# A 4-byte write per partition put between two large loads on the SyncE queue of an RMSNorm kernel

## The chip, the cores and the metric

One core of one Trainium2 chip. The metric is device time in microseconds (us) of one execution, median of the runs. A kernel's profile is one execution; its "span" is counted from the first to the last instruction and is about 1.9 us shorter than the time. All profiles told of here are of the undisturbed ("fast") state, with a granted TensorE clock of 1.0.

Engines: ACT is ScalarE, DVE is VectorE, PE is TensorE, SP is SyncE, POOL is GpSimd. An "SPq" line is the sequencer of SyncE, which issues the DMAs of this kernel. The DMA work itself is done by 16 DMA engines.

Three words are used throughout. A "piece" is one contiguous run of elements in a DMA; the profile counts one packet for each. The "ring" of a DMA engine is the list of packets that it works through. A DMA has "landed" when the trace shows the semaphore event of its completion.

## The reference

```python
x: (16, 1024, 512) float32, gamma: (512,) float32
rms = sqrt(mean(x ** 2, axis=-1, keepdims=True) + 1e-5)
out = x / rms * gamma
```

33.55 MB come in and 33.55 MB go out. The 16384 rows are cut into 4 tiles; in a tile each of the 128 partitions holds 32 whole rows (64 KB, contiguous in memory).

## The kernel before

Three slots of 64 KB per partition; tiles 0, 1, 2 have a slot each and tile 3 uses slot 0 again after tile 0 is stored. All large DMAs are on the SyncE queue.

```python
    def load(t, slot, r0, r1):
        nc.sync.dma_start(out=slots[slot][:, r0:r1], in_=xv[t][:, r0:r1])
    def store(t, slot, r0, r1):
        nc.sync.dma_start(out=ov[t][:, r0:r1], in_=slots[slot][:, r0:r1])

    load(0, 0, 0, 16)
    load(0, 0, 16, 32)
    load(1, 1, 0, 32)
    load(2, 2, 0, 32)
    # ... (gamma broadcast over the partitions, eps) cut
    # compute(slot, r0, r1), per 8 rows: ACT squares (and sums half of the groups itself,
    # the other half through PSUM and a DVE reduce, L74), ACT sqrt, DVE reciprocal,
    # then 8 DVE scalar_tensor_tensor (L88), one per row: slot = slot * rstd * gamma. Cut.
    compute(0, 0, 32)
    store(0, 0, 0, 32)
    compute(1, 0, 16)
    store(1, 1, 0, 16)
    load(3, 0, 0, 16)
    load(3, 0, 16, 32)
    compute(1, 16, 32)
    store(1, 1, 16, 32)
    compute(2, 0, 32)
    store(2, 2, 0, 32)
    compute(0, 0, 16)
    store(3, 0, 0, 16)
    compute(0, 16, 32)
    store(3, 0, 16, 32)
```

## Time and profile before

| | before |
|---|---|
| time, median (lowest to highest) of the first three runs | 162.51 us (162.43 to 162.78) |
| span of the profile | 160.6 us |
| DVE busy, ACT busy | 123.4 us (77%), 79.9 us (50%) |
| share of the 16 DMA engines' span used by the SyncE queue | 97.9% |

From the page of the kernel before: the count of DMA packets, the queues (packets, MB, share of 16 engines), and the chain of work that ended last, as shares of the span.

```profile
span 160.6 us, 402 instructions
PE 2.0 (1%) x2; PEld 0.5 (0%) x2; DVE 123.4 (77%) x163; ACT 79.9 (50%) x162; POOL 0.2 (0%) x4
...
DMA packets 1732, 67.13 MB, mean 418 GB/s; under 512 B 193, under 2 KB 193, under 8 KB 194
## 3 DMA queue, kind: packets, MB, share of 16 engines
q1 hardware_dynamic: 1728, 67.11, 97.9%
...
DVE 71%; ACT 12%; DMA 8%; issue 1%; DVEq 0%
```

The chain says DVE and the queue table says DMA. Both are nearly full, which is why neither may be read alone. The next view is the timeline of SyncE's issues before (start, us from the first to the end of the last of a merged group, engine and line, what, how many).

```profile
0.73 1.95 SPq L42 DMA_DIRECT2D slot<-in_x_dram  x4
50.09 23.33 SPq L45 DMA_DIRECT2D out_dram<-slot  x2
82.24 0.84 SPq L42 DMA_DIRECT2D slot<-in_x_dram  x2
88.31 59.93 SPq L45 DMA_DIRECT2D out_dram<-slot  x4
```

All four loads are queued by 2.7 us, store(0) follows at 50.1 us, and the last store is issued at about 147.9 us (88.31 + 59.93, less its own 0.34). The landing times in the trace's semaphore events show one unbroken stream: 12.80 and 22.48 us for the halves of load(0), 41.84 for load(1), 62.83 for load(2), 82.17 for store(0), and so on to 149.89 and 159.55 for the last two stores. Store(0) was issued at 50.1 us and found the engines busy with load(2) until 62 us.

The last view is of ACT between 22 and 60 us before: only the instructions ahead of which ACT stood idle; in brackets, for how long, and what ended it.

```profile
39.26 0.30 ACT L85 ACTIVATE rms<-ss,eps_t 128x8 f32<-128x8 f32 x1 [5.76 <-DVE ss L74]
41.86 0.63 ACT L79 ACTIVATE sq_scratch<-slot 128x512 f32<-128x512 f32 x1 [2.30 <-DMA slot<-in_x_dram]
52.30 1.88 ACT L73 ACTIVATE sq<-slot 128x2048 f32<-128x2048 f32 x1 [4.88 <-DVE ss L74]
```

ACT waits for load(1) at 41.86 us. Afterwards it waits another 4.88 us for DVE. So load(1) could come up to about 4.9 us later and only shorten that second wait. This is the slack of load(1).

### The profile page before, as it was taken

How to read it: one execution, taken by the hardware profiler on the slowest of the kernel's cores; microseconds unless marked ns; L12 is line 12 of the kernel's file. 1: busy time of each engine (PE TensorE's matmuls, PEld its weight loads, DVE VectorE, ACT ScalarE, POOL GpSimd, SP SyncE). 2: the span in 40 equal slices, each digit the busy share in tenths (PEclk: the TensorE clock that was granted, in tenths of full speed). 3: DMA queues.
4: the chain of work that ended last, by engine and by line, in shares of the span. 5: the costliest groups of instructions: out<-in, count | busy, mean ns of one | idle time of the engine just before them, and what ended most of it. 6: DMA issues, size and time to landing. Idle time of an engine off the chain costs nothing.

```text
span 160.6 us, 402 instructions
## 1 busy us (share of the span) xinstructions
PE 2.0 (1%) x2; PEld 0.5 (0%) x2; DVE 123.4 (77%) x163; ACT 79.9 (50%) x162; POOL 0.2 (0%) x4
## 2 busy tenths in 40 slices
PE   4000000000000000000000000000000000000000
PEld 1000000000000000000000000000000000000000
DVE  0101909999999509999999999998999999998000
ACT  3008999930580999995099314003998960000000
POOL 0000000000000000000000000000000000000000
DMA  7999999969969997997999999999997997999993
GB/s 262 392 408 498 400 408 506 522 261 522 522 263 522 506 278 345 441 522 310 473 392 416 465 416 416 473 416 408 457 547 310 506 490 310 416 465 408 433 457 155
DMA packets 1732, 67.13 MB, mean 418 GB/s; under 512 B 193, under 2 KB 193, under 8 KB 194
## 3 DMA queue, kind: packets, MB, share of 16 engines
q1 hardware_dynamic: 1728, 67.11, 97.9%
q14 instruction: 2, 0.02, 0.0%
q10 hardware_dynamic: 2, 0.00, 0.0%
HBM read 33.56 MB, written 33.55 MB: 418 GB/s over the span
## 4 chain that ended last, share of the span: by engine, by line
DVE 71%; ACT 12%; DMA 8%; issue 1%; DVEq 0%
DVE slot L88 52%; DVE ss L74 18%; DMA slot<-in_x_dram 8%; ACT sq_scratch L79 6%; ACT sq L73 4%; DVE rstd L86 1%; ACT L85 1%; ACT rms L85 1%; DVEq L136 0%
## 5 line engine op out<-in xcount | busy, mean ns | idle before, releaser
L88 DVE SCALAR_TENSOR_TENSOR slot<-slot,rstd,gamma_b 128x512 f32<-128x512 f32 x128 | 85.7, 746 | 0.1
L79 ACT ACTIVATE sq_scratch<-slot 128x512 f32<-128x512 f32 x64 | 40.0, 625 | 13.9 <-DMA slot<-in_x_dram 12.6
L74 DVE TENSOR_REDUCE ss<-sq 128x4 f32<-128x2048 f32 x16 | 36.1, 2276 | 10.5 <-ACT sq L73 10.4
L73 ACT ACTIVATE sq<-slot 128x2048 f32<-128x2048 f32 x16 | 29.8, 1860 | 4.9 <-DVE ss L74 4.9
L85 ACT ACTIVATE rms<-ss,eps_t 128x8 f32<-128x8 f32 x16 | 4.4, 297 | 37.4 <-DVE ss L74 37.2
L79 ACT ACTIVATION_READ_ACCUMULATOR sq_scratch<-slot 128x1 f32 x64 | 11.9, 187 | 0.0
L86 DVE RECIPROCAL rstd<-rms 128x8 f32<-128x8 f32 x16 | 2.8, 188 | 9.8 <-ACT rms L85 9.8
L59 DVE COPY gamma_b<-sq 128x512 f32<-128x512 f32 x1 | 0.7, 692 | 3.2 <-PE sq L57 3.2
L57 PE MATMUL sq<-gamma_row,ones_col 1*128 1x512 f32 x2 | 2.0, 1122 | 2.2 <-DMA gamma_row<-in_gamma_dram 2.2
L79 ACT ACT_TABLE_LOAD x1 | 1.3, 1283 | 1.3 <-PEq L125 1.3
L85 ACT ACT_TABLE_LOAD x1 | 1.3, 1283 | 0.0
L55 DVE MEMSET ones_col<- 1x128 f32 x1 | 0.2, 165 | 0.8 <-PEq L125 0.8
L57 PEld LDWEIGHTS sq<-gamma_row,ones_col 1*128 1x128 f32 x2 | 0.5, 305 | 2.1 <-issue 2.1
L125 POOL MEMSET const-bfloat16-1.0<- 128x1 bf16 x1 | 0.1, 102 | 0.0
L125 POOL MEMSET const-uint8-127<- 128x1 uint8 x1 | 0.1, 102 | 0.0
L125 POOL MEMSET const-float32-0.0<- 128x1 f32 x1 | 0.1, 99 | 0.2 <-issue 0.2
L125 POOL MEMSET const-float32-1.0<- 128x1 f32 x1 | 0.1, 99 | 0.0
L62 DVE MEMSET eps_t<- 128x1 f32 x1 | 0.1, 59 | 0.0
## 6 DMA issues: line engine op xcount, KB each, us to landing
slot<-in_x_dram SPq DMA_DIRECT2D x4, 4096.0 KB, 19.3
out_dram<-slot SPq DMA_DIRECT2D x4, 4096.0 KB, 18.0
slot<-in_x_dram SPq DMA_DIRECT2D x2, 50.5
out_dram<-slot SPq DMA_DIRECT2D x2, 27.6
gamma_row<-in_gamma_dram ACTq DMA_DIRECT2D x1, 2.0 KB
```

The source lines that it names most:

```text
L55: nc.vector.memset(ones_col, 1.0)
L57: nc.tensor.matmul(gamma_psum[:, 0], ones_col, gamma_row, start=True, stop=True)
L59: nc.vector.tensor_copy(out=gamma_b, in_=gamma_psum[:, 0])
L62: nc.vector.memset(eps_t, eps)
L73: nc.scalar.activation(out=sq, in_=slots[slot][:, g + h : g + h + H, :], func=AF.Square)
L74: nc.vector.tensor_reduce(out=ss[:, h : h + H], in_=sq, axis=mybir.AxisListType.X, op=OP.add)
L79: nc.scalar.activation(out=sq_scratch, in_=slots[slot][:, g + r, :], func=AF.Square, accum_out=ss[:, r : r + 1],)
L85: nc.scalar.activation(out=rms, in_=ss, func=AF.Sqrt, bias=eps_t, scale=1.0 / D)
L86: nc.vector.reciprocal(out=rstd, in_=rms)
L88: nc.vector.scalar_tensor_tensor(out=slots[slot][:, g + r, :], in0=slots[slot][:, g + r, :], scalar=rstd[:, r : r + 1], in1=gamma_b, op0=O ...
L125: nc = _bacc.Bacc("TRN2", target_bir_lowering=False, num_devices=1)
```

## The change

One constant element (0.0) is written to the first element of each partition's first row of `out`, on the SyncE queue, behind the loads of the first tile and ahead of the second's. store(0) overwrites all of it later, so the result is the same. It adds work and removes none; a reason for it could be to touch `out` early.

```diff
     load(0, 0, 0, 16)
     load(0, 0, 16, 32)
+    nc.sync.dma_start(out=ov[0][:128, 0, 0:1], in_=nc.const_aps.tensor(0.0, [128, 1], fp32), allow_slow_non_contiguous=True)
     load(1, 1, 0, 32)
     load(2, 2, 0, 32)
```

The order of the instructions on PE, ACT, DVE and POOL is the same in both kernels. SyncE has one issue more, and the DMA semaphores are shared out one place further.

## The prediction

> **What bounds the kernel now.** Two things nearly tie. The DMA queue table gives the SyncE queue (q1) 97.9% of the 16 engines' span, and the windows table shows 419 to 433 GB/s in nearly every stretch of 5 us. In the DMA packet records each engine runs its packets back to back from about 1.7 us to 158.5-159.2 us of a 160.6 us span (32 KB took 1.213 us, 64 KB 2.418 us, 27.1 GB/s an engine, 434 GB/s for 16; the Trainium skill, "DMA: Bandwidth & Descriptors", "Where 436 GB/s comes from", states 435, and this trace agrees). The landings are one stream: load(0) halves 12.8 and 22.5 us, load(1) 41.8, load(2) 62.8, store(0) 82.2, and so on to 159.6. The second bound is VectorE: the chain of waits is DVE 71% of the span, DVE is busy almost without a pause from 24 to 147.9 us, and the last store is issued at 147.9. The last 12.7 us is that store. When it reached the DMA engines, four of 16 had been idle 0.06 to 0.2 us; the other twelve were still finishing the store before it. So DMA leads by a hair.
>
> **What the change adds.** One DMA of 128 pieces of 4 B, 8 pieces on each engine, queued behind load(0) and ahead of load(1). No instruction of ACT, DVE, PE or POOL moves; on SyncE one issue is added (0.34 to 0.58 us each in the timeline) far ahead of need. Semaphores shift by one: store(0) also waits for the little write, done long before; load(3)'s first half also waits for a semaphore that gamma used, done too. No new late wait. store(0) overwrites the elements, so the result stands.
>
> **Cost.** The trace has no small HBM write. Its 4 B semaphore packets take 9 ns, the 2 KB gamma packet 98 ns. An estimate from these is 8 x (9 to 60) ns = 0.1 to 0.5 us on each ring. The skill (same page, "Specifications") says that below 512 B the DMA does read-modify-write; no run here shows it yet. If each piece waited out a memory round trip it would be several us; I give that little chance.
>
> A possible gain: the last packet of load(2) on every engine took 3.4 to 3.95 us instead of 2.42, just as the first store's packets come up (58-61.5 us), and the later change from load to store (110 us) shows nothing. If that is a cost of the first write to out, the little write meets it at 22 us instead. I expect it to move, not vanish. If it vanished, the last store is still released by DVE at 147.9, so at most about 0.7 us is gained (159.2 down to 158.5).
>
> **On the critical path.** load(1) may come 4.9 us later before it hurts compute (ACT stalls 4.9 us on DVE afterwards, at 52.3 us), load(2) more. But the rings hold a backlog all the way, so ring time added at 22 us arrives one for one at the end: +0.1 to 0.5 us.
>
> **Prediction.** 162.7 us, 80% range 161.7 to 164.0. Faster by over 2%: 0.02; within 2%: 0.91; slower by over 2%: 0.07.
>
> **What would show it.** Little packets at about 22 us, under 0.5 us per engine in sum; load(1) and all later landings up to 140 us shifted by the same 0.1 to 0.5 us; DVE times from 24 to 147.9 us unchanged within 0.1 us; the long packets at 58 us gone and a similar stall at 22 us.
>
> **What would make it wrong.** Small writes served one by one at a memory round trip (stream moves by several us; beyond 4.9 us DVE slips too); the stall at 58 us vanishing for nothing; the small write upsetting the even spread over engines.

## The result

| | before | after |
|---|---|---|
| time, median (lowest to highest) of 4 runs | 162.58 us (162.43 to 162.78) | 162.40 us (162.33 to 162.87) |
| ratio after / before | | 0.9994, 95% interval 0.9972 to 1.0017: same |
| span of the profile | 160.6 us | 160.6 us |

Ratios here and below are the mean time of one kernel's fast runs over that of the other's fast runs of the same rounds, so they are not quite the ratio of the medians quoted. A second job of the changed kernel with more rounds is told under the experiments.

The same lines of the page, after:

```profile
span 160.6 us, 403 instructions
PE 2.0 (1%) x2; PEld 0.5 (0%) x2; DVE 123.4 (77%) x163; ACT 80.0 (50%) x162; POOL 0.2 (0%) x4
...
DMA packets 1876, 67.13 MB, mean 418 GB/s; under 512 B 337, under 2 KB 337, under 8 KB 338
## 3 DMA queue, kind: packets, MB, share of 16 engines
q1 hardware_dynamic: 1872, 67.11, 97.8%
...
DVE 71%; ACT 12%; DMA 7%; issue 1%; DVEq 0%
```

The reader should see 144 more packets, all under 512 B: 128 pieces of 4 B and 16 semaphore writes, that is 8 and 1 on each engine. SyncE's issues and ACT's waits, after:

```profile
0.73 0.86 SPq L42 DMA_DIRECT2D slot<-in_x_dram  x2
1.64 0.42 SPq L49 DMA_DIRECT2D out_dram<-const-float32-0.0  x1
2.11 1.03 SPq L42 DMA_DIRECT2D slot<-in_x_dram  x2
50.08 23.35 SPq L45 DMA_DIRECT2D out_dram<-slot  x2
...
39.25 0.30 ACT L86 ACTIVATE rms<-ss,eps_t 128x8 f32<-128x8 f32 x1 [5.75 <-DVE ss L75]
41.87 0.63 ACT L80 ACTIVATE sq_scratch<-slot 128x512 f32<-128x512 f32 x1 [2.31 <-DMA slot<-in_x_dram]
52.28 1.88 ACT L74 ACTIVATE sq<-slot 128x2048 f32<-128x2048 f32 x1 [4.86 <-DVE ss L75]
```

The extra issue takes 0.42 us of SyncE, 19 us before the DMA engines come to it; nothing waits for it. In the packet records each of the small packets took 9 ns, 0.08 us for the 9 of one engine. The little write landed at 22.66 us, 0.17 us behind the second half of load(0), and load(1) at 41.85 us, against 41.84 before. ACT's wait behind it is 4.86 us instead of 4.88.

One thing in the packet records answers to a claim of the prediction. Packets of 64 KB take 2.418 us each, but before the change the last packet of load(2) on every engine, which starts at about 58 us, took 1.33 us longer on average (0.95 to 1.53 us on single engines), just as store(0) comes up behind it. After the change it is 1.21 us longer, at the same place, and no packet near 22 us is lengthened. The stall was not moved by the little write.

### The profile page after: what moved, and what is told of

Its sections match the earlier page's. It is cut to its first block, busy times and chain, and to the rows that moved or that the text cites. A ratio compares the mean times of both kernels' runs of the same rounds, so it can differ in the third digit from the quotient of the medians.

```text
span 160.6 us, 403 instructions
## 1 busy us (share of the span) xinstructions
PE 2.0 (1%) x2; PEld 0.5 (0%) x2; DVE 123.4 (77%) x163; ACT 80.0 (50%) x162; POOL 0.2 (0%) x4
## 4 chain that ended last, share of the span: by engine, by line
DVE 71%; ACT 12%; DMA 7%; issue 1%; DVEq 0%
DVE slot L89 52%; DVE ss L75 18%; DMA slot<-in_x_dram 7%; ACT sq_scratch L80 6%; ACT sq L74 4%; DVE rstd L87 1%; ACT L86 1%; ACT rms L86 1%; DVEq L137 0%
```

## The experiments

Theory A, after the result: the stream of DMA packets is packed from end to end, and the write costs its ring time of 0.08 us. Rivals: the write is hidden because DMA has slack; or small writes cost much more than 9 ns, and the first few were only hidden. All kernels gave the right result except the last, which is wrong. Each job also ran the kernel before on the same chip; its medians were 162.61 (first job), 162.73 (second) and 162.52 us (third).

### a1_after_again: the changed kernel again

No edit.

> The changed kernel again, in more rounds. Theory A (a backlogged DMA stream; the little write costs its ring time of 9 packets x 9 ns = 0.08 us per engine, as the trace of after shows): 162.5 to 162.7 us, ratio 1.000 to 1.002. Rival B (the little write changes the stream for the better or worse by something that the packets do not show): a ratio off 1 by more than 0.3%. The long last packets of load(2) at 58 us stay.

Measured: 162.47 us (6 runs) against 162.61 us, ratio 0.9992, interval 0.9977 to 1.0006. Load(1) landed at 41.84 us. The long last packets of load(2) were there (1.22 us over). So the write changes nothing down to about 0.2%.

### e5_head: the same write ahead of the first load

```diff
+    nc.sync.dma_start(out=ov[0][:128, 0, 0:1], in_=nc.const_aps.tensor(0.0, [128, 1], fp32), allow_slow_non_contiguous=True)
     load(0, 0, 0, 16)
     load(0, 0, 16, 32)
```

> The same little write of one element per row, ahead of the first load instead of behind it. Theory A: the first load is issued one SyncE issue (0.42 us in the trace of after) later, so both the DMA stream and the chain of ACT and DVE begin 0.4 us later, and the total is 162.9 to 163.1 us; position matters, not the write itself. Rival: the write is free anywhere, 162.5 us.

Measured: 162.86 us, ratio 1.0019 (1.0005 to 1.0033). SyncE's issues in this kernel:

```profile
0.72 0.37 SPq L47 DMA_DIRECT2D out_dram<-const-float32-0.0  x1
1.15 1.92 SPq L42 DMA_DIRECT2D slot<-in_x_dram  x4
50.68 23.33 SPq L45 DMA_DIRECT2D out_dram<-slot  x2
```

The first load is issued at 1.15 instead of 0.73 us, its first half landed at 13.40 instead of 12.80 us, and DVE released store(0) 0.6 us later. The total rose by 0.25 us between the medians, less than the 0.4 us expected, with the sign expected. Of the two places tried, the added issue cost something at the head, where the first load waits behind it, and nothing measurable behind load(0). The first half came 0.60 us later and the issue accounts for 0.42 us of that; the rest is not explained.

### e1_dose32 and e2_dose128: more pieces in the same place

```diff
+    nc.sync.dma_start(out=ov[0][:128, 0, 0:64:2], in_=nc.const_aps.tensor(0.0, [128, 32], fp32), allow_slow_non_contiguous=True)
```

(and `0:256:2` with `[128, 128]` in e2). Every second element is written, so each is a piece of 4 B: 256 and 1024 pieces on each engine.

> 32 elements per row in place of one: 256 pieces of 4 B on each engine. Theory A (ring time, 9 ns apiece, backlog until the end): 256 x 9 ns = 2.3 us of packets on each engine at 22 us; load(1) lands at 44.1 instead of 41.85 us; DVE times unchanged (slack of 4.9 us); everything in the stream up to the last store 2.2 us later; total 162.5 + 2.2 = 164.7 us. Rival C (DVE alone bounds the kernel, DMA has slack): stays at 162.5 us. Rival D (small writes beyond a few are served at a memory round trip, the first 8 were only hidden): much more than 2.3 us, over 10 us.

> 128 elements per row: 1024 pieces of 4 B on each engine. Theory A: 1024 x 9 ns = 9.2 us; load(1) lands at 51.0 us, past the 4.9 us of slack, so DVE slips by about 4 us too; total 162.5 + 9.1 = 171.6 us, set by DMA. Rival C: only the DVE slip, 162.5 + 4.2 = 166.7 us. Rival D: over 190 us.

Measured: 189.47 us for e1 (ratio 1.166) and 253.92 us for e2 (1.557). Theory A's figure of 9 ns a piece fell, by a factor of ten: load(1) landed 28.8 us later in e1 (70.61 us) and 92.6 us later in e2 (134.47 us). Rival D holds in its direction. In the records the earliest 1024 small packets of the 16 engines together still took 9 ns; from the 2049th on the mean over the next 2048 was 0.15 to 0.17 us, with single ones over 2 us. So a record of 9 ns does not give the cost of a small write. That it says only how soon the engine went on to the next packet is my reading and not shown.

### e7_rows31: 248 pieces per engine, each in a row of its own

```diff
+    nc.sync.dma_start(out=ov[0][:, 0:31, 0], in_=nc.const_aps.tensor(0.0, [128, 31], fp32), allow_slow_non_contiguous=True)
```

> 248 pieces of 4 B on each engine as in e1_dose32 (256), but one element in each of 31 rows that are 2 KB apart, not 32 elements in one 256 B stretch. e1 cost 27 us, some 0.1 us a piece, while the 8 pieces of the change cost 9 ns each. Theory B (each engine takes a small number of short writes without waiting, after that each piece is served at about 0.1 us, wherever it goes): again 24 to 29 us over before, 187 to 191 us. Rival S (neighbouring pieces collide in the same stretch of memory, and the change was cheap because its pieces lie 64 KB apart): 248 x 9 ns = 2.2 us, 164 to 166 us.

Measured: 172.14 us, 9.4 us over the median of before. Neither figure was met. The place matters (e1, with about as many pieces side by side, cost 26.9 us), and 248 pieces 2 KB apart still cost four times the 2.2 us of the rival. Load(1) landed 10.75 us later.

### e8_dose8 and e11_dose16: looking for the edge

```diff
+    nc.sync.dma_start(out=ov[0][:128, 0, 0:16:2], in_=nc.const_aps.tensor(0.0, [128, 8], fp32), allow_slow_non_contiguous=True)
```

(and `0:32:2` with `[128, 16]` in e11): 64 and 128 pieces per engine.

> 8 elements per row: 64 pieces of 4 B on each engine, at the edge. In e1, e2 and e7 the first 1024 pieces over all 16 engines took 9 ns each, the next ones on average 30 ns and more, so theory B puts the capacity near 64 pieces an engine. If so: 64 x 9 ns = 0.6 us of stream, all pieces at 9 ns, load(1) at 42.4 us, total 162.5 to 163.1 us. If the capacity is well under 64 or the pieces are paid late (by the loads behind them): load(1) several us late, total 164 us or more.

> 16 elements per row: 128 pieces on each engine, past the edge. Theory B, with 95 to 145 ns for each piece over 64 as in e2 and e1: stream 6 to 9 us later at load(1), of which the stall at 58 us gives back about 1.3 us: total 167 to 170.5 us. Without an edge (a cost for each piece from the first on): e8 and e11 would stand in the ratio of 1 to 2.

Measured: 165.14 us for e8 (ratio 1.0158, 1.0127 to 1.0189) and 173.19 us for e11 (1.065). So 64 pieces per engine are not free, though all but 2 of the 1232 small packets in the SyncE queue of e8 are recorded at 9 ns (the two at 13 ns). The cost stands on the packets behind them: the first 64 KB packets of load(1) took 3.39 us longer on average over the 16 engines, and load(1) landed at 45.67 us, 3.83 us late. My belief in free room for 64 pieces fell; e11 came out above its range. The increases were 2.6 and 10.7 us, a ratio of 4 rather than 2, so the cost is not in proportion to the count either.

e8 also tests the slack of load(1). The page's count of packets (1024 + 16 more than before), SyncE's issues of the write and of load(1) and load(2), and ACT's waits in e8:

```profile
DMA packets 2772, 67.13 MB, mean 411 GB/s; under 512 B 1233, under 2 KB 1233, under 8 KB 1234
...
1.62 0.70 SPq L49 DMA_DIRECT2D out_dram<-const-float32-0.0  x1
2.36 17.40 SPq L42 DMA_DIRECT2D slot<-in_x_dram  x2
...
26.41 0.63 ACT L80 ACTIVATE sq_scratch<-slot 128x512 f32<-128x512 f32 x1 [2.31 <-DMA slot<-in_x_dram]
39.42 0.30 ACT L86 ACTIVATE rms<-ss,eps_t 128x8 f32<-128x8 f32 x1 [3.36 <-DVE ss L75]
45.70 0.63 ACT L80 ACTIVATE sq_scratch<-slot 128x512 f32<-128x512 f32 x1 [5.97 <-DMA slot<-in_x_dram]
52.46 1.88 ACT L74 ACTIVATE sq<-slot 128x2048 f32<-128x2048 f32 x1 [1.21 <-DVE ss L75]
```

The second issue line shows something that the packets do not: of its 17.40 us, 14.94 us are the issue of load(1) alone, which took 0.55 us with the change (more on this below the table). Compare the last two lines with those of before: ACT waits 3.67 us longer for load(1) and 3.67 us less for DVE, and goes on at 52.46 instead of 52.30 us. The slack was real and took the delay. The total still rose by 2.6 us, because the DMA stream itself was late: the last store landed at 162.36 instead of 159.55 us. A delay of the stream is paid at the end of the stream, whether or not a compute engine waited for it in between.

### e9_contig32: eight pieces of 128 B

```diff
+    zeros = const.tile([P, 32], fp32)
+    nc.gpsimd.memset(zeros, 0.0)
     load(0, 0, 0, 16)
     load(0, 0, 16, 32)
+    nc.sync.dma_start(out=ov[0][:, 0, 0:32], in_=zeros)
```

> The same stretch per row filled with one run of 128 B: 8 pieces on each engine, 32 times the bytes of the change. Theory B (count of pieces): as cheap as the change, 162.4 to 162.8 us. Rival (any write shorter than 512 B is served slowly): over 163 us. The long last packets of load(2) stay or go: see e4.

Measured: 162.37 us (2 runs), ratio 0.998 (0.994 to 1.001); load(1) at 41.97 us. As many bytes per row as e1's elements, in 8 pieces per engine instead of 256, and the 26.9 us are gone. So it is the count of pieces that costs, together with their place (e7), and not the bytes; a single short run per partition is cheap at 4 B and at 128 B.

The pieces set side by side ("load(1) late" is its landing time less the 41.84 us of before; "time" is the difference of the medians of one job):

| kernel | pieces per engine | where | load(1) late | time |
|---|---|---|---|---|
| after (two traces) | 8 of 4 B | one per partition | 0.01 and 0.00 us | -0.18 and -0.14 us |
| e9 | 8 of 128 B | one per partition | 0.13 us | -0.36 us |
| e8 | 64 of 4 B | 8 side by side | 3.83 us | +2.62 us |
| e11 | 128 of 4 B | 16 side by side | 12.88 us | +10.67 us |
| e7 | 248 of 4 B | 31 rows of 2 KB | 10.75 us | +9.41 us |
| e1 | 256 of 4 B | 32 side by side | 28.77 us | +26.86 us |
| e2 | 1024 of 4 B | 128 side by side | 92.63 us | +91.31 us |

A rival to "the small writes are slow" was not tested: that the loads behind them came late because SyncE issued them late. With many pieces SyncE is held in the issue of load(1): for 14.94 us in e8, 20.2 in e11, 20.8 in e7, 25.0 in e1 and 95.8 us in e2. In e8 this is not the cause, since that issue ended at 17.31 us and the DMA engines came to the pieces only at 21.69 us. In the four others it ended after the engines had come to them (22.57, 23.21, 27.34 and 98.20 us, against about 22 us), and in e11 the recorded busy share of the 16 engines fell to 0.41 between 24 and 26 us. So in these four a share of the cost may be late issue. Nor does any run separate the reading of a piece from its writing. So a cost per piece in this document is a cost of such a DMA as a whole.

In all five kernels with 64 pieces or more the stall of load(2)'s last packets at the switch to store(0) was gone, which gives back up to 1.3 us; the next experiments are about that stall.

### e4_early_store, e10_early_4rows and e3_split_store0: the stall at 58 us

e4 stores one row of zeros per partition in the place of the little write (8 pieces of 2 KB per engine), e10 four rows (8 pieces of 8 KB):

```diff
+    zeros = const.tile([P, D], fp32)          # e10: [P, 4 * D]
+    nc.gpsimd.memset(zeros, 0.0)
     load(0, 0, 0, 16)
     load(0, 0, 16, 32)
+    nc.sync.dma_start(out=ov[0][:, 0], in_=zeros)
+    # e10: out=ov[0][:, 0:4].rearrange("p r d -> p (r d)")
```

e3 has no little write, and issues store(0) in two halves, the first one early:

```diff
-    store(0, 0, 0, 32)
+    store(0, 0, 0, 16)
+    store(0, 0, 16, 32)
```

> A real early store in the place of the little write: one 2 KB row per partition, 8 pieces on each engine. Ring time 8 x about 0.08 us = 0.6 us, so load(1) lands at 42.5 us and the total is 162.7 to 163.2 us. On the long last packets of load(2) at 58 us (1.2 to 1.3 us over 2.418 on average over the engines), which the change did not move: theory F (cost of the first real store of the program) has them normal here, with a like stall at 22 us; theory L (they are tied to how soon the store behind them was issued, 11.5 us before its turn) has them unchanged.

> No little write; store(0) in two halves, the first issued as soon as its rows are done (about 35 us). Theory L: the store now stands in the ring over 20 us before its turn at 61 us, the last packets of load(2) are normal, the stream runs 1.2 us earlier and the total falls by at most 0.7 us (the last store is released by DVE at 147.9 us): 161.8 to 162.3 us. Theory F: the stall of 1.2 us stays, 162.5 us.

> An early store of 4 rows (8 KB per partition, 64 KB per engine = 2.4 us of ring time) in the place of the little write, so few pieces but a stream 2.4 us later. In the runs so far the excess of the last packets of load(2) falls as the stream comes later: 1.33 us (before), 1.21, 0.84 (stream 0.64 us later), 0.55 (stream 0.98 us later), 0 (stream 10 us later). Theory T (the stall ends at a nearly fixed time, about 62 us, so a later stream loses less there): no stall here, load(2) ends about 1.1 us later than before, total 163.4 to 163.9 us. Theory F (cost of the first stores, paid once): a stall of 0.5 to 1.3 us stays or moves to 22 us, everything 2.4 us later, 164.7 to 165.2 us.

Measured: e4 162.83 us, ratio 1.0009 (0.9986 to 1.0033); e3 162.95 us, 1.0017 (0.9990 to 1.0044); e10 165.07 us, 1.0145 (1.0119 to 1.0172). The excess over the normal packet time, averaged over the engines, from the packet records:

| kernel | last packets of load(0), at 18 to 22 us, ahead of the early write | last packets of load(2), at about 58 us, ahead of store(0) |
|---|---|---|
| before | 0 | 1.33 us |
| after, and again | 0, 0 | 1.21, 1.22 us |
| e3 | 0 | 1.06 us |
| e9 | 0 | 1.04 us |
| e5 | 0 | 0.84 us |
| e6 (below) | 0 | 0.5 us, and 0.9 us spread over the packets from 28 to 56 us |
| e4 | 0.30 us | 0.55 us |
| e10 | 1.19 us | 0.05 us |

In e3 the first half of store(0) was issued at 34.88 us, with 27 us to its turn, and the stall stayed: it is not a matter of a store issued too late (theory L fell). In e10 the stall is gone at 58 us and stands at 22 us instead, ahead of the early store, in the same form: the last packets of the load in front are lengthened. The total came out in the range of theory F and 1.2 us over that of theory T. So a wait of about 1.2 us came once, ahead of the first sizeable store, at both places where such a store was put, and not at later switches from load to store (in the kernel before, all the large packets behind load(2) together exceed their normal time by under 0.1 us per engine). e4's small store took over part of it. The 4 B write of the change takes over next to none. Size alone is not the rule, though: 64 or more 4 B pieces per engine also left nothing at 58 us. Nor is theory T wholly out: it fits the smaller excess of e5, but not the stall of e10 at 22 us. What the wait is made of, and why e5 and e4 add up to only about 0.85 us, stays open. e6 is the same kernel as before up to 110 us and had its stall spread differently, so single traces differ here by some tenths of a us.

### e6_less_dma: does DMA or DVE bound the kernel?

```diff
-    store(2, 2, 0, 32)
+    store(2, 2, 0, 16)
```

> Wrong result on purpose: the second half of store(2) is left out, 4.19 MB or 9.65 us less in the stream, no engine's work changed. By the near tie read from before (last store released by DVE at 147.9 us, its DMA work done by 158.5 us at the earliest): total falls by at most 0.7 us, to 161.8 to 162.4 us, and the DMA engines stand idle ahead of the last store for some us. Rival (DMA alone bounds the kernel): 9 us less, 153 us.

Measured: 161.80 us, ratio 0.9948 (0.9927 to 0.9968); the result is wrong in the rows not stored. Taking 9.65 us of work out of the DMA stream gained 0.7 us. The two windows ahead of the last store, before and then in e6 (columns: window, its length, busy time with counts of PE, PEld, DVE, ACT and POOL, clock, DMA share, GB/s):

```profile
140.00:145.00 5.00, 0.00 (x0) 0.00 (x0) 4.96 (x9) 0.00 (x0) 0.00 (x0) 1.00 0.99 426
145.00:150.00 5.00, 0.00 (x0) 0.00 (x0) 2.88 (x5) 0.00 (x0) 0.00 (x0) 1.00 1.00 433
```

```profile
140.00:145.00 5.00, 0.00 (x0) 0.00 (x0) 4.96 (x9) 0.00 (x0) 0.00 (x0) 1.00 0.49 210
145.00:150.00 5.00, 0.00 (x0) 0.00 (x0) 2.84 (x5) 0.00 (x0) 0.00 (x0) 1.00 0.42 177
```

DVE is as busy as before, while the DMA share fell to half: DMA now stands idle and the last store waits for DVE. So DVE's bound lies 0.7 us below that of DMA. The kernel is held by both, and DMA's bound is the later one.

No experiment pointed to a version that beats both kernels by more than this 0.7 us, since the bytes cannot be fewer, and none was run.

## Why the prediction was right

- **The time.** 162.7 us with 161.7 to 164.0 was predicted, 162.40 us measured (162.47 in the second job).
- **No new wait.** Right: the landings and the waits of ACT and DVE agree to 0.03 us up to 52 us, and the one new issue costs 0.42 us on SyncE, 19 us ahead of need. e5 shows where that issue would have cost something.
- **Two bounds that nearly tie, DMA ahead.** Right, shown by e6: at most 0.7 us to gain was predicted, 0.7 us was gained when 9.65 us of DMA work was taken out.
- **"Ring time added at 22 us arrives one for one at the end."** Right in kind and not exact: e8 delayed load(1) by 3.83 us and the last landing by 2.81 us, because the stall at 58 us went away in between. e4 delayed load(1) by 0.98 us and the last landing by 0.49 us.
- **The slack of load(1), 4.9 us.** Right: e8 used 3.67 us of it and DVE went on 0.16 us later.
- **0.1 to 0.5 us for the 8 pieces.** Too high, and from the wrong source. I took the 9 ns of a semaphore packet for the low end. The records of the change show that 9 ns, yet e8 shows that it does not measure the cost of a small write: with 64 pieces nearly all recorded at 9 ns, load(1) came 3.83 us late. If one counts the stall of 1.3 us as paid there too, that is (3.83 - 1.3) / 64 = 0.04 us a piece, and at that rate 8 pieces would be 0.3 us. Two traces show 0.01 us or less, and the last store landed 0.09 and 0.05 us later than before. So a few pieces per engine do go unseen; how many, between 8 and 64, was not measured. To this extent the prediction was lucky: the same reckoning at 64 pieces gave 0.6 us where load(1) came 3.83 us late, and it held for the change because 8 pieces were few enough, which no number in the trace of before could show.
- **"The long packets at 58 us gone and a similar stall at 22 us."** Wrong. The step was: "If that is a cost of the first write to out, the little write meets it at 22 us instead. I expect it to move, not vanish." The first write alone did not bring it: with the change 1.21 us stood at 58 us as before and nothing at 22 us, while the 8 KB per partition of e10 moved it (1.19 us at 22 us, 0.05 us at 58 us). How much has to be written lies between the two and is not known. The mistake had no effect on the total of the change.

The Trainium skill, "DMA: Bandwidth & Descriptors", section "Specifications", names read-modify-write below 512 B. No run here shows a read-modify-write as such. The runs agree with the page that short writes are slow, but only by number: 64 or more per engine cost 0.04 to 0.1 us each, 8 per engine nothing that could be measured.

## What to carry to other kernels

A DMA of one short piece per partition cost nothing measurable in this kernel when it stood behind loads that were already queued, and about 0.25 us ahead of the first load; ask how many pieces each DMA engine gets, not how few bytes there are. Look at how long SyncE is held by the issue behind such a DMA, too. A packet's recorded time is not the cost of a small write: look at how much longer the next large packet takes and when it lands. Where the DMA stream is packed from end to end, compute slack protects the compute engines and not the total, so read the landing of the last store as well as the waits.

## What the Trainium skill lacked or had wrong

- "DMA: Bandwidth & Descriptors", "Specifications" gives 512 B as the least size for full rate, and no figure for how many short writes go unseen: 8 of 4 B per engine moved the next load's landing by 0.01 us, 64 by 3.83 us, 1024 by 92.6 us (90 ns each, late issue included).
- The same page, "Why small descriptors are slow (HBM only)", puts the penalty down to a fixed cost per packet and per descriptor. That says nothing of the place, and in the runs the cost per piece depends on it: 248 pieces 2 KB apart cost 9.4 us, 256 side by side 26.9 us.
- I found no page that has the wait ahead of the first sizeable store behind a stream of loads: 1.2 to 1.3 us on average over the engines, once, and none at the switch at 110 us.
- I found no page that says that small writes can hold back the completion of a load queued ahead of them: in e8 the second half of load(0) landed at 26.39 us instead of 22.48 us, though its packets ended at about 22.3 us, and ACT waited 2.31 us for it. In e11 it landed at 28.49 us, but in e7 and e1 at 22.60 and 22.68 us, so the number of pieces alone does not decide it.
- I found no page that says that a DMA of many pieces holds SyncE in the issue behind it: 0.55 us with 8 pieces per engine, 14.94 us with 64, 95.8 us with 1024.
